# Own buffers for weight sums, the wide down group run from the last row pair to the first, and a fifth place for split weights

## The chip, the cores and the metric

The kernel runs on one core of a Trainium2 chip. The metric is the device time of one execution in microseconds. PE is the matrix engine, PEld its weight load, DVE the vector engine, ACT the scalar engine, POOL is GpSimd, SP the queue from which nearly all loads are issued.

## The reference, cut to what matters

One encoder block: RMSNorm, a combined input projection, two kinds of attention, an output projection with a residual, RMSNorm, and a gated MLP with a residual. All of it is float32. The change touches the MLP alone (256 tokens, `D_MODEL` 2048, `D_FF` 5632):

```
g = x @ w_gate
u = x @ w_up
gc = conv_b + sum over i of conv_w[i] * shifted g
return (jax.nn.silu(gc) * u) @ w_down
```

## The kernel before, in words

**Split weights.** Each float32 weight block is cut into a high part, which ACT writes (`whi`, operations of line 250), and a low part, which DVE writes (`wlo = weight - whi`, line 254). PE then multiplies each block two or three times (high by high, low by high, high by low). A split weight stands in a *place*: one `whi` tile and one `wlo` tile of 128x1024. There are four places (`his`, `los`, lines 320 and 321), filled in turn, and a place is free again when PE has used it. So ACT, DVE and PE form a pipeline: ACT writes the high part of a piece, DVE the low part behind it, PE uses both.

**Raw weights.** They come from DRAM by SP into buffers of the pool `raws` (line 319): five tiles `raw`, later one `more_raw` (line 1879), and, as the activations `hl` die, eight halves of the tiles `halves0` to `halves3` (`hl_free`, line 740). A buffer is free again when the low parts of all that it holds are written.

**Row pairs.** The MLP's down projection runs for most columns by a scheme with seven products for each 2x2 block of tiles. `RowPair` (line 376) is one such block row: its weights, and sums of its weight quarters, are multiplied with the activations (`act`) or with sums of activation quarters (`S`, "sums of values"). The weight sums are made by DVE into a buffer of `raws` (`weight_sums`, line 613; `sums`, `two` and `more` in the code), which is claimed in `load_pair` (line 575) together with the buffers of the loads. The values' sums `S` are made on DVE and ACT when the activations are finished (`value_sums`, line 1954), saved to DRAM (`save_sums`, line 1974) and loaded again into `sin0`, `sin1` or `sums0` (the pool `s_parts`) by `load_S` (line 560) before the pair needs them. Part of the weight sums of the wide group is made in DRAM long before by accumulating DMAs (`early0` to `early21`) and loaded like weights.

**The stages.** Attention fills the first 400 us or so. Then come gate and up tiles, part of them in five groups of the seven-product scheme ("quads" below, weights `w_up_s`); then the "mid" group (`w_down_m`, 22 row pairs, 512 columns); then the "wide" group (`w_down_s`, 22 row pairs, 1024 columns, four pieces a pair), from 948 us on. Between the pieces of the wide group stand pieces of four more column tiles of `w_down` ("others"). Both groups need the values' sums of all 22 pairs, so each is loaded from DRAM twice; only those of the last two pairs go from their making straight to the mid group.

**What sets the order.** Each engine runs its instructions in the order in which they were written out. A planner at build time writes them: threads (the functions with `yield`) claim buffers from pools (`Slots`), wait for events, and are served by modelled costs. `LANDING` (line 67) is the planner's constant for how long a load takes to land. The planner's times decide nothing at run time; only the order that comes out, and the waits that the shared buffers bring, do.

**Outputs.** `mid_out` (line 2194) ends the mid group: DVE combines seven banks into a buffer, ACT scales, POOL adds the residual (line 278), POOL issues two stores. `down_out` (line 2008) does the like for each of the four other column tiles, in two tiles `mt` of the pool `mts` (12 tiles of 128x258), from which POOL stores. `scheme_out` (line 2233) ends the kernel.

Of the kernel before, what the change touches and what calls it, by code (L numbers as in the profile page):

```python
# [15 lines left out]
P = 128  # L16
# [49 lines left out]
COPY_PACE, COPY_AT, SUMS_AT = 6000.0, 14, 48  # L66
LANDING, SAVING = 2600.0, 2500.0
BEHIND = 3
MID_LEAD, TAIL = 4, "mmdmmddddmmddd"
LAST = FC // 2 - 1  # L70
# [147 lines left out]
def encoder_block(ctx: ExitStack, tc: tile.TileContext, io):  # L218
# [11 lines left out]
    def tiles(pool, n, shape, name, dt=F32):  # L230
        return [pool.tile(shape, dt, tag=f"{name}{i}", name=f"{name}{i}") for i in range(n)]
# [90 lines left out]


    combined = Slots(tiles(wpool, 1, [P, PW], "sums"))

# [50 lines left out]
    class RowPair:  # L376
# [50 lines left out]
        def used(self, kind):  # L427
            self.left[kind] -= 1
            if self.left[kind] == 0:
                fl.put(raws, self.at[kind])  # L430

    s_parts = Slots([])
    pieces = []
# [125 lines left out]
    def load_pair(r):  # L559
        def load_S():  # L560
            if r.near:
                r.ev_S = ev_near[r.g]
                return
            if r.of == "mid" and r.g in last_S:
                yield last_S[r.g][1]
                r.S = last_S[r.g][0][0]
                fl.set(r.ev_S)
                return
            r.S = yield from one(s_parts)
            src, saved = saved_sums["up" if r.of == "up" else "down"][r.g]  # L570
            yield saved
            yield "sp", 600
            load(r.S, src, r.ev_S, nc.sync)

        q = r.q
        if r.wide:
# [36 lines left out]
    def weight_sums(r):  # L613
        yield r.loaded
        q = r.q
        if r.wide:
            low, up, t, m = (r.at[k] for k in ("lower", "upper", "two", "more"))
            if r.mode == "both":
                yield r.summed[0]
                yield from TT(m[:, :q], low[:, :q], t[:, :q], ALU.add)  # L620
                yield from TT(m[:, q:], m[:, :q], low[:, q:], ALU.add)
                fl.set(r.summed[1])
                r.used("two")
            else:
                yield r.first_loaded
# [1246 lines left out]
    near, ev_near = [None] * (KC // 2), [Event() for _ in range(KC // 2)]  # L1872
    act = mts = None

    def mlp_buffers():

        nonlocal act, mts
        yield ev_s2t
# [3 lines left out]
        act = mpool.tile([P, FC, 2, SEQ], F32R, name="act")  # L1882
        mts = Slots(tiles(mpool, 12, [P, NT], "mt"))
        for t in tiles(mpool, 2, [P, PW], "sin"):
            fl.put(s_parts, t)
        for t in tiles(mpool, 1, [P, PW], "more_raw"):
            fl.put(raws, t)
        for b in banks[4:]:
# [65 lines left out]
    def value_sums(dst, saved, a, b, place=None):  # L1954
# [152 lines left out]
    def scheme_products(p, r):  # L2107
# [31 lines left out]
        if p is r.pieces[-1]:  # L2139
            if not r.near:  # L2140
                if r.S is not near[-1]:
# [302 lines left out]
```

## Time and profile before

| what | value |
|---|---|
| time, median of 3 runs | 1107.14 us (1105.82 to 1108.59) |
| the profiled execution | 1107.99 us |
| its span, first to last instruction | 1106.0 us |
| granted TensorE clock | 1.000 |
| DVE busy in the span | 1016.9 us (92%) |
| ACT busy | 750.8 us (68%) |
| POOL busy | 149.6 us (14%) |
| loads, stores and copies | 265.35 MB, mean 240 GB/s |

The profile is a page of one execution and the views that its trace answers: busy times in chosen stretches, waits (who waited for whom), a timeline of single instructions, and the DMAs from issue to landing. In a row of the timeline the columns are start and duration in us, engine, line of the code, operation, output and inputs by the program's names without their numbers, shape, and a count where equal rows were merged; in brackets stands idle time ahead of it, with what ended it. Starts are the better measure of pace: an instruction's shown duration overlaps the next one's by some 0.1 us on DVE, and by 0.17 us on PE.

### The profile page before, as it was taken

Reading aid. Unit: us, or ns where it says so; the run is one execution under the profiler, and the core shown is the slowest. Engines: PE = TensorE matmul, PEld = TensorE weight load, DVE = VectorE, ACT = ScalarE, POOL = GpSimd, SP = SyncE. Lnnn points to the kernel's source line nnn. Section 1 sums busy time; section 2 is a strip of 40 time slices with the busy share of each in tenths; the row PEclk is TensorE's granted clock in tenths of the full one; section 3 lists DMA queues with packets and bytes.
Section 4 is the critical chain, followed back from the end, with each engine's and each line's share of the span. In section 5 each row is a group of like instructions: output and inputs, shape, how many; then the busy total and the mean of one; then the engine's idle time right before and its main releaser. Section 6 shows DMA issues by size and latency. Waiting matters only on the chain.

```text
span 1106.0 us, 22349 instructions
## 1 busy us (share of the span) xinstructions
PE 1095.7 (99%) x8164; PEld 1046.2 (95%) x8164; DVE 1016.9 (92%) x1922; ACT 750.8 (68%) x1514; POOL 149.6 (14%) x217
## 2 busy tenths in 40 slices
PE   9999999999999999999999999999999999999998
PEld 9999999999999999999999999999999999887777
DVE  8979888888878989999999999999999998999997
ACT  8788979798647776656656666665666665766664
POOL 3211222322433400000000000000000000304011
PEclk9999999999999999999999999999999999999999
DMA  8765678667877887665747668667888879699891
GB/s 325 253 230 175 194 226 228 173 195 183 257 204 209 237 283 270 213 205 184 255 161 227 208 208 276 216 220 258 277 307 295 286 260 359 233 337 318 274 313 62
DMA packets 82470, 265.35 MB, mean 240 GB/s; under 512 B 9304, under 2 KB 13016, under 8 KB 82360
## 3 DMA queue, kind: packets, MB, share of 16 engines
q1 hardware_dynamic: 78600, 254.08, 67.6%
q0 software_dynamic: 3472, 9.57, 5.4%
q8 instruction: 64, 1.05, 0.4%
q14 instruction: 46, 0.38, 0.1%
q10 hardware_dynamic: 288, 0.27, 0.1%
HBM read 245.39 MB, written 35.13 MB: 254 GB/s over the span
## 4 chain that ended last, share of the span: by engine, by line
PE 83%; DVE 7%; ACT 4%; DMA 3%; issue 2%; POOL 0%; DVEq 0%; SPq 0%; ACTq 0%; POOLq 0%
PE bank L290 23%; PE bank L713 15%; PE bank L714 15%; PE bank L715 15%; PE bank L2040 10%; PE bank L2041 5%; DVE wlo L254 4%; PE bank L296 2%; ACT whi L250 1%; DMA raw<-early 1%; DVE scr L262 1%; ACT scr L250 1%; DMA raw<-in_w_cq 1%; DMA halves<-early 1%; DVE halves L254 1%
## 5 line engine op out<-in xcount | busy, mean ns | idle before, releaser
L250 ACT ACTIVATE whi<-raw 128x512 fp32r<-128x512 f32 (+2 forms) x513 | 383.0, 767 | 152.4 <-PE bank L714 48.7
L254 DVE TENSOR_TENSOR wlo<-raw,whi 128x512 fp32r<-128x512 f32 (+2 forms) x513 | 445.1, 886 | 29.1 <-ACT whi L250 25.4
L713 PE MATMUL bank<-hl,whi 128*128 128x258 f32 (+1 forms) x1208 | 347.7, 288 | 0.0
L714 PE MATMUL bank<-hl,whi 128*128 128x258 f32 (+1 forms) x1208 | 343.7, 285 | 0.0
L715 PE MATMUL bank<-hl,wlo 128*128 128x258 f32 (+1 forms) x1208 | 343.3, 284 | 0.2
L715 PEld LDWEIGHTS bank<-hl,wlo 128*128 128x128 f32 x1208 | 229.7, 190 | 1.0 <-DVE wlo L254 0.6
L714 PEld LDWEIGHTS bank<-hl,whi 128*128 128x128 f32 x1208 | 229.3, 190 | 0.1
L713 PEld LDWEIGHTS bank<-hl,whi 128*128 128x128 f32 x1208 | 228.3, 189 | 0.4
L290 PE MATMUL bank<-whi,act 128*128 128x256 f32 (+1 forms) x600 | 152.9, 306 | 0.0
L2040 PE MATMUL bank<-hl,whi 128*128 128x512 f32 x384 | 136.5, 395 | 0.0
L290 PEld LDWEIGHTS bank<-whi,act 128*128 128x128 f32 x600 | 105.0, 189 | 6.2
L2041 PE MATMUL bank<-hl,wlo 128*128 128x256 f32 x384 | 107.6, 280 | 0.0
L278 POOL TENSOR_TENSOR mt<-mt,mt 128x256 f32<-128x256 f32 x3 | 13.5, 4496 | 646.6 <-ACT mt L250 646.6
L290 PE MATMUL bank<-wlo,act 128*128 128x256 f32 (+1 forms) x300 | 91.7, 306 | 0.0
L2040 PEld LDWEIGHTS bank<-hl,whi 128*128 128x128 f32 x384 | 72.1, 188 | 14.8
L250 ACT ACTIVATE whi<-halves 128x1024 fp32r<-128x1024 f32 (+1 forms) x68 | 62.4, 933 | 34.1 <-PE bank L290 16.7
L290 PE MATMUL bank<-whi,sin 128*128 128x256 f32 (+1 forms) x264 | 76.3, 333 | 0.0
L254 DVE TENSOR_TENSOR wlo<-halves,whi 128x1024 fp32r<-128x1024 f32 (+1 forms) x68 | 72.9, 1099 | 2.9 <-ACT whi L250 2.8
L2041 PEld LDWEIGHTS bank<-hl,wlo 128*128 128x128 f32 x384 | 72.4, 189 | 0.0
L250 ACT ACTIVATE whi<-more_raw 128x1024 fp32r<-128x1024 f32 (+2 forms) x58 | 49.9, 871 | 25.1 <-PE bank L714 9.3
L290 PEld LDWEIGHTS bank<-wlo,act 128*128 128x128 f32 x300 | 56.7, 189 | 2.8
L254 DVE TENSOR_TENSOR wlo<-more_raw,whi 128x1024 fp32r<-128x1024 f32 (+2 forms) x58 | 57.0, 994 | 2.4 <-ACT whi L250 2.4
(311 smaller groups left out, 2163.1 us busy)
## 6 DMA issues: line engine op xcount, KB each, us to landing
raw<-in_w_gate SPq DMA_DIRECT2D x74, 512.0 KB, 4.8
raw<-in_w_in SPq DMA_DIRECT2D x52, 512.0 KB, 4.9
raw<-in_w_up SPq DMA_DIRECT2D x43, 512.0 KB, 4.9
raw<-in_w_up_s SPq DMA_DIRECT2D x34, 512.0 KB, 4.4
raw<-in_w_out SPq DMA_DIRECT2D x32, 512.0 KB, 5.3
sin<-s_down SPq DMA_DIRECT2D x30, 512.0 KB, 6.5
s_down<-sums SPq DMA_DIRECT2D x22, 512.0 KB, 4.4
raw<-in_w_down_m SPq DMA_DIRECT2D x18, 512.0 KB, 5.5
```

The costliest lines, as they stand in the source:

```text
L250: nc.scalar.activation(out, in_, f, **kw)
L254: nc.vector.tensor_tensor(out, a, b, op)
L262: nc.vector.scalar_tensor_tensor(out, a, s, b, op0, op1)
L278: nc.gpsimd.tensor_tensor(out, a, b, op)
L290: nc.tensor.matmul(o, l, r, start=start, stop=stop)
L296: nc.tensor.transpose(o, i, ident[:n, :n])
L713: nc.tensor.matmul(ps, whi, xhi, start=start, stop=False)
L714: nc.tensor.matmul(ps, whi, xlo, start=False, stop=False)
L715: nc.tensor.matmul(ps, wlo, xhi, start=False, stop=stop)
L2040: nc.tensor.matmul(ps, whi, x, start=start, stop=False)
L2041: nc.tensor.matmul(ps[:, :n], wlo, x[:, 0, :], start=False, stop=stop)
```

## The change

1. **Own buffers for weight sums.** A new pool `made` takes `more_raw` and the two halves of `halves3`; `raws` keeps the five `raw` tiles and the other six halves. The sums' buffers are claimed from `made` when DVE is to make the sums, and no longer from `raws` when the pair's load is planned. The number of buffers is the same.
2. **The wide group runs from pair 21 to pair 0**, and the values' sums of pairs 19, 20 and 21, which the mid group used last, stay on chip for the wide group's first three pairs. Three loads of `s_down` and two saves go away, 512 KB each.
3. **A fifth place.** The 12 tiles `mt` are cut from three tiles of four. Behind `mid_out`, `mts_to_ring` takes all 12, gives four back, and turns the other two tiles into a fifth `whi` and a fifth `wlo` (`whi_more`, `wlo_more`). In the wide group, `down_out` has four `mt` where it had twelve.
4. `LANDING` in the planner goes from 2600 to 3200 ns.

The counts of computing instructions stay the same on every engine. PE's order is the same up to the first wide product; from there on the pairs come in the other order, and the others' pieces stand at somewhat other points among them.

The planner writes all engines' orders anew, and three places show what that does. In the rows, `waits` names the engines or DMA queues whose semaphores a row waits for (DMAHW are SP's transfers, DMASW POOL's), numbers behind a name tell buffers apart, and the instruction's line is one higher after the change.

The first place is DVE in the fourth quad, around the low part `wlo1` of a pair. Before:

```order
L254 TENSOR_TENSOR wlo0_89<-raw1_81,whi0_85 128x1024 [waits PE_49,Activation_49]
L254 TENSOR_TENSOR more_raw0_5458<-raw0_80 128x512 [waits DMAHW6_49]
L254 TENSOR_TENSOR more_raw0_5458<-raw0_80,more_raw0_5458 128x256 [waits DVE_49]
L254 TENSOR_TENSOR more_raw0_5458<-more_raw0_5458,raw0_80 128x256 [waits DVE_49]
L254 TENSOR_TENSOR wlo1_90<-raw4_84,whi1_86 128x1024 [waits DMAHW4_49,Activation_49]
L254 TENSOR_TENSOR wlo2_91<-raw0_80,whi2_87 128x512 [waits PE_49,Activation_49]
L254 TENSOR_TENSOR wlo2_91<-raw0_80,whi2_87 128x256 [waits PE_49,Activation_49]
L254 TENSOR_TENSOR sums0_93<-mt5_5449,sums0_93 128x256 [waits DMAHW5_49]
```

And with the change:

```order
L255 TENSOR_TENSOR wlo0_89<-more_raw0_5449,whi0_85 128x1024 [waits PE_49,Activation_49]
L255 TENSOR_TENSOR sums0_93<-mt1_5445,sums0_93 128x256 [waits DMAHW5_49,Activation_49]
L255 TENSOR_TENSOR more_raw0_5449<-raw0_80 128x512 [waits DMAHW6_49,DVE_49]
L255 TENSOR_TENSOR more_raw0_5449<-raw0_80,more_raw0_5449 128x256 [waits DVE_49]
L255 TENSOR_TENSOR more_raw0_5449<-more_raw0_5449,raw0_80 128x256 [waits DVE_49]
L255 TENSOR_TENSOR wlo1_90<-raw1_81,whi1_86 128x1024 [waits DMAHW4_49,Activation_49]
L255 TENSOR_TENSOR wlo2_91<-raw0_80,whi2_87 128x512 [waits PE_49,Activation_49]
L255 TENSOR_TENSOR wlo2_91<-raw0_80,whi2_87 128x256 [waits PE_49,Activation_49]
```

A row of `value_sums` (`sums0<-mt`) has moved from behind the three low parts to ahead of them. The same stands in the second and third quad.

The second place is DVE in the wide group, from the row that frees a buffer for a load of `early` sums to the row that reads that load. Before, for pair 16: the low part from `halves1` in the first row frees it, SP's load of `early16` goes into it, and the last row reads it.

```order
L254 TENSOR_TENSOR wlo1_90<-halves1_11086,whi1_86 128x1024 [waits Activation_49]
L254 TENSOR_TENSOR wlo2_91<-more_raw0_5458,whi2_87 128x1024 [waits DMAHW4_49,Activation_49]
L254 TENSOR_TENSOR wlo3_92<-raw0_80,whi3_88 128x512 [waits Activation_49]
L254 TENSOR_TENSOR halves0_11043<-raw3_83 128x512 [waits DMAHW4_49,DMAHW3_49]
L254 TENSOR_TENSOR halves0_11043<-halves0_11043,raw1_81 128x512 [waits DMAHW1_49,DVE_49]
L254 TENSOR_TENSOR wlo0_89<-raw2_82,whi0_85 128x1024 [waits Activation_49]
L254 TENSOR_TENSOR wlo1_90<-raw4_84,whi1_86 128x512 [waits DMAHW7_49,Activation_49]
L254 TENSOR_TENSOR halves3_11164<-halves0_11043,raw1_81 128x512
L254 TENSOR_TENSOR more_raw0_5458<-halves3_11164,halves1_11086 128x512 [waits DMAHW6_49,DMAHW1_49]
```

With the change, the pair whose load has the fewest rows between is pair 5. The row ahead of these twelve (a low part from `halves1`) frees the buffer, and the last one reads it:

```order
L255 TENSOR_TENSOR wlo1_90<-halves2_11117,whi1_86 128x512 [waits DMAHW4_49,Activation_49]
L255 TENSOR_TENSOR more_raw0_5449<-halves3_11155,raw0_80 128x512
L255 TENSOR_TENSOR wlo2_91<-raw1_81,whi2_87 128x1024 [waits Activation_49]
L255 TENSOR_TENSOR wlo3_92<-raw3_83,whi3_88 128x1024 [waits DMAHW6_49,Activation_49]
L255 TENSOR_TENSOR wlo_more_11455<-halves3_11155,whi_more_11454 128x1024 [waits Activation_49]
L255 TENSOR_TENSOR wlo0_89<-raw0_80,whi0_85 128x1024 [waits Activation_49]
L255 TENSOR_TENSOR wlo1_90<-halves2_11117,whi1_86 128x1024 [waits Activation_49]
L255 TENSOR_TENSOR wlo2_91<-halves3_11155,whi2_87 128x1024 [waits Activation_49]
L255 TENSOR_TENSOR halves3_11155<-halves0_11034 128x512 [waits DMAHW6_49,DMAHW3_49,DVE_49]
L255 TENSOR_TENSOR halves3_11155<-halves3_11155,halves0_11034 128x512 [waits DVE_49]
L255 TENSOR_TENSOR wlo3_92<-more_raw0_5449,whi3_88 128x512 [waits PE_49,Activation_49]
L255 TENSOR_TENSOR more_raw0_5449<-halves1_11078 128x512 [waits DMAHW3_49,DMAHW2_49,DVE_49]
```

Eight rows lay between freeing and reading, counted with the reading one; now it is twelve, and twelve to 23 for the other pairs from 18 down. Before, the pairs 14, 16, 18, 19 and 21 had eight to ten.

The third place is DVE where the fifth place is first filled, nine rows behind the last one of `mid_out`'s combination of the banks:

```order
L255 TENSOR_TENSOR wlo0_89<-raw2_82,whi0_85 128x1024 [waits Activation_49]
L255 TENSOR_TENSOR wlo1_90<-halves0_11034,whi1_86 128x512 [waits DMAHW0_49,Activation_49]
L255 TENSOR_TENSOR more_raw0_5449<-halves3_11155,halves1_11078 128x512
L255 TENSOR_TENSOR wlo2_91<-halves0_11034,whi2_87 128x1024 [waits Activation_49]
L255 TENSOR_TENSOR wlo3_92<-raw4_84,whi3_88 128x1024 [waits DMAHW2_49,Activation_49]
L255 TENSOR_TENSOR wlo_more_11455<-halves3_11155,whi_more_11454 128x1024 [waits DMASW6_49,Activation_49,Pool_49]
L255 TENSOR_TENSOR wlo0_89<-halves1_11078,whi0_85 128x1024 [waits Activation_49]
```

The row of `wlo_more` waits for POOL and for the POOL queue's store of the first `down_out` (DMASW6), which reads from the `mt` tiles that become the place. Such a wait did not stand here before.

The core of the diff:

```diff
-LANDING, SAVING = 2600.0, 2500.0
+LANDING, SAVING = 3200.0, 2500.0
+RING_AT = 5
+    made = Slots([])
...
-                fl.put(raws, self.at[kind])
+                by_sums = kind in ("more", "sums") or kind == "two" and self.mode == "third"
+                fl.put(made if by_sums else raws, self.at[kind])
...
-        for g in range(FC // 2):
+        order = range(FC // 2) if of == "mid" else range(LAST, -1, -1)
+        for g in order:
             r = RowPair(src[g], g, q, of)
-            r.first, r.last, r.near = g == 0, g == LAST, False
+            r.first, r.last, r.near = g == order[0], g == order[-1], False
...
+            if r.of == "down" and r.g > LAST - 3:
+                yield ev_kept[r.g]
+                r.ev_S = kept_S[r.g].ev_S
+                r.S = kept_S[r.g].S
                 return
...
-            r.at["two"], r.at["more"] = yield raws, 2
             if r.mode == "both":
+                r.at["two"] = yield from one(raws)
...
-            r.at["raw"], r.at["sums"] = yield raws, 2
+            r.at["raw"] = yield from one(raws)
...
+            if r.mode == "both":
+                yield r.summed[0]
+                r.at["more"] = yield from one(made)
+            else:
+                yield r.first_loaded
+                r.at["two"], r.at["more"] = yield made, 2
...
-        t, raw = r.at["sums"], r.at["raw"]
+        t = r.at["sums"] = yield from one(made)
...
-            fl.put(raws, t[:, a : a + PW])
+            fl.put(raws if 2 * i + a // PW < 8 - 2 else made, t[:, a : a + PW])
...
-        mts = Slots(tiles(mpool, 12, [P, NT], "mt"))
+        mt_rows[:] = tiles(mpool, 3, [P, 4 * NT], "mt")
+        mts = Slots([t[:, i * NT : (i + 1) * NT] for t in mt_rows for i in range(4)])
...
-        fl.spawn(save_sums(dst, saved, parts, place is None and not last))
+        if not last:
+            fl.spawn(save_sums(dst, saved, parts, place is None))
...
+    def mts_to_ring():
+        yield mts, 12
+        yield scheme[RING_AT][0].ready[0]
+        for i in range(4):
+            fl.put(mts, mt_rows[0][:, i * NT : (i + 1) * NT])
+        for i, (slots, name) in enumerate(((his, "whi_more"), (los, "wlo_more"))):
+            t = mpool.tile([P, 4 * NT], F32R, tag=f"mt{i + 1}", name=name)
+            fl.put(slots, t[:, :PW])
...
+        fl.spawn(mts_to_ring())
```

More of the change, by code (lines that the diff above doesn't have):

```diff
@@ L429, in used @@
             if self.left[kind] == 0:
-                fl.put(raws, self.at[kind])
-    s_parts = Slots([])
+                by_sums = kind in ("more", "sums") or kind == "two" and self.mode == "third"
+                fl.put(made if by_sums else raws, self.at[kind])
+    s_parts, kept_S = Slots([]), {}
+    ev_kept = {g: Event() for g in range(LAST - 2, LAST + 1)}
     pieces = []
@@ L567, in load_S @@
                 fl.set(r.ev_S)
+                kept_S[r.g] = r
+                fl.set(ev_kept[r.g])
+                return
+            if r.of == "down" and r.g > LAST - 3:
+                yield ev_kept[r.g]
+                r.ev_S = kept_S[r.g].ev_S
+                r.S = kept_S[r.g].S
                 return
             r.S = yield from one(s_parts)
+            if r.of == "mid" and r.g > LAST - 3:
+                assert r.S is not near[-1]
+                kept_S[r.g] = r
+                fl.set(ev_kept[r.g])
             src, saved = saved_sums["up" if r.of == "up" else "down"][r.g]
@@ L616, in weight_sums @@
         if r.wide:
+            if r.mode == "both":
[4 more added lines that the diff above has]
+                r.at["two"], r.at["more"] = yield made, 2
             low, up, t, m = (r.at[k] for k in ("lower", "upper", "two", "more"))
             if r.mode == "both":
-                yield r.summed[0]
                 yield from TT(m[:, :q], low[:, :q], t[:, :q], ALU.add)
@@ L624, in weight_sums @@
             else:
-                yield r.first_loaded
                 yield from TT(m[:, :q], up[:, :q], up[:, q:], ALU.add)
@@ L633, in weight_sums @@
             return
-        t, raw = r.at["sums"], r.at["raw"]
+        t = r.at["sums"] = yield from one(made)
+        raw = r.at["raw"]
         if r.mode == "third":
@@ L1872, in encoder_block @@
     near, ev_near = [None] * (KC // 2), [Event() for _ in range(KC // 2)]
-    act = mts = None
+    act = mts = mpool = None
+    mt_rows = []
     def mlp_buffers():
-        nonlocal act, mts
+        nonlocal act, mts, mpool
         yield ev_s2t
@@ L1886, in mlp_buffers @@
         for t in tiles(mpool, 1, [P, PW], "more_raw"):
-            fl.put(raws, t)
+            fl.put(made, t)
         for b in banks[4:]:
@@ L2140, in scheme_products @@
             if not r.near:
-                if r.S is not near[-1]:
+                if kept_S.get(r.g) is r:
+                    pass
+                elif r.S is not near[-1]:
                     fl.put(s_parts, r.S)
```

## The prediction

> **What bounds the kernel now.** I read the stretches first: busy time of each engine in chosen windows (core, window, length, then PE, PEld, DVE, ACT and POOL with their counts, the granted clock, the DMA share and GB/s).
>
> ```profile
> 640.00:720.00 80.00, 80.00 (x640) 78.47 (x639) 78.72 (x146) 50.22 (x81) 0.00 (x0) 1.00 0.70 233
> 800.00:900.00 100.00, 100.00 (x751) 95.98 (x750) 92.31 (x162) 61.01 (x96) 0.00 (x0) 1.00 0.83 286
> 900.00:948.00 48.00, 48.00 (x318) 43.91 (x318) 43.95 (x71) 28.04 (x42) 3.35 (x4) 1.00 0.88 319
> 948.00:1000.00 52.00, 52.00 (x241) 42.43 (x240) 51.77 (x58) 37.02 (x45) 12.86 (x8) 1.00 0.85 301
> 1000.00:1025.00 25.00, 24.29 (x116) 19.78 (x115) 24.86 (x28) 15.58 (x17) 7.09 (x4) 1.00 0.93 314
> 1025.00:1050.00 25.00, 23.88 (x114) 19.46 (x113) 22.60 (x26) 14.81 (x16) 0.00 (x0) 1.00 0.79 271
> 1050.00:1075.00 25.00, 22.84 (x111) 18.33 (x110) 23.27 (x26) 15.85 (x20) 5.33 (x4) 1.00 0.89 300
> ```
>
> PE is full up to 1000 us at a granted clock of 1.00, so nothing can be won there, only lost. From 1000 to 1075, in the wide group, it is not, while DVE is busy 99% of one window and has holes in the next two. So PE and DVE bound this stage together. Next I read who waited: PE from 780 us on, then DVE from 940 us on.
>
> ```profile
> PE bank L290 <- DVE wlo L254: 4.0, 5, 1.1
> ```
>
> ```profile
> DVE more_raw L254 <- DMA halves<-early: 2.3, 1, 2.3
> DVE halves L254 <- DMA raw<-early: 1.5, 1, 1.5
> ```
>
> PE waits for the low parts five times, and DVE waits twice for a load of `early` sums. The timeline shows the five, and that DVE's two waits stand in front of two of them.
>
> ```profile
> 1037.31 0.69 DVE L254 TENSOR_TENSOR halves<-halves,raw 128x512 f32<-128x512 f32 x1
> 1040.30 0.69 DVE L254 TENSOR_TENSOR more_raw<-halves,halves 128x512 f32<-128x512 f32 x1 [2.30 <-DMA halves<-early]
> ```
>
> ```profile
> 1054.18 0.69 DVE L254 TENSOR_TENSOR halves<-raw,raw 128x512 f32<-128x512 f32 x1 [1.51 <-DMA raw<-early]
> ```
>
> ```profile
> 1010.89 0.50 PE L290 MATMUL bank<-wlo,sin 128*128 128x512 f32 x1 [0.71 <-DVE wlo L254]
> ```
>
> ```profile
> 1040.44 0.39 PE L290 MATMUL bank<-whi,act 128*128 128x512 f32 x1
> 1040.66 0.39 PE L290 MATMUL bank<-whi,sums 128*128 128x512 f32 x1
> 1042.18 0.50 PE L290 MATMUL bank<-wlo,sums 128*128 128x512 f32 x1 [1.12 <-DVE wlo L254]
> ```
>
> ```profile
> 1056.07 0.50 PE L290 MATMUL bank<-wlo,sin 128*128 128x512 f32 x1 [1.08 <-DVE wlo L254]
> ```
>
> ```profile
> 1065.86 0.51 PE L290 MATMUL bank<-wlo,sin 128*128 128x512 f32 x1 [0.55 <-DVE wlo L254]
> 1068.74 0.50 PE L290 MATMUL bank<-wlo,sin 128*128 128x512 f32 x1 [0.53 <-DVE wlo L254]
> ```
>
> Undisturbed, a matmul starts about 0.22 us behind the one ahead (1040.44 to 1040.66) though it is shown 0.39 long. A bracket thus hides 0.17 us, and the five cost 4.0 + 5 x 0.17 = 4.85 us. That is all the change can win; PE's work does not change.
>
> **The change part by part.**
>
> *Loads earlier (own buffers for sums).* The load that DVE waits for at 1040.30 was issued here:
>
> ```profile
> 1032.62 0.33 SPq L543 DMA_DIRECT2D halves<-early  x1
> ```
>
> It landed 7.7 us later; in before's order only eight DVE rows lie between the row that frees its buffer and the one that reads it. From 948 to 1000 DVE does 58 rows in 51.77 us, 0.89 us each, so eight rows are 7.1 us: too few. With the change at least twelve rows lie between, an estimate of 10.7 us by the same 0.89, and most loads have more. The two DMA waits should go, and with them the stalls at 1042.18 and 1056.07: 1.12 + 1.08 + 2 x 0.17 = 2.54 us. What is late next is DVE itself.
>
> *DVE's own lag.* The other three stalls cost 0.71 + 0.55 + 0.53 + 3 x 0.17 = 2.3 us. Each stands behind adds on POOL; the first has no DMA wait ahead of it at all:
>
> ```profile
> 994.58 0.69 DVE L254 TENSOR_TENSOR halves<-halves 128x512 f32<-128x512 f32 x1
> 995.18 1.82 DVE L254 TENSOR_TENSOR wlo<-raw,whi 128x1024 fp32r<-128x1024 f32 x2
> ...
> 1002.67 0.68 DVE L254 TENSOR_TENSOR more_raw<-halves,halves 128x512 f32<-128x512 f32 x1
> 1003.39 1.11 DVE L254 TENSOR_TENSOR more_raw<-more_raw,halves 128x512 f32<-128x512 f32 x1
> ```
>
> ```profile
> 993.79 10.16 POOL L278 TENSOR_TENSOR mt<-mt,mt 128x256 f32<-128x256 f32 x1 [34.09 <-ACT mt L250]
> 1004.03 1.08 POOL L278 TENSOR_TENSOR mt<-mt,s 128x256 f32<-128x256 f32 x1
> ```
>
> A sum of this shape takes 0.68, but 1.11 beside POOL's add. The change leaves these POOL adds where they are. It also makes more DVE rows wait for the row just ahead of them: nine more in the wide stage, because three buffers serve all sums. Such a row starts 0.72 us behind (1002.67 to 1003.39) instead of 0.60 (994.58 to 995.18), so nine cost 9 x 0.12 = 1.1 us. Against it stands the fifth place: DVE and ACT can run one split further ahead, about 1.1 us. Also, the last two stalls, 9 and 12 us behind the one at 1056.07, met a lead that the DMA waits had used up. Bounds of what remains: 0 us, and 2.3 + 1.1 = 3.4 us. I take 1.3, nearer the lower end, since two of the three stalls lose part of their cause.
>
> *Fewer transfers.* Three loads of `s_down` and two saves, 512 KB each, vanish: 2.6 MB.
>
> ```profile
> sin<-s_down SPq DMA_DIRECT2D x30, 512.0 KB, 6.5
> s_down<-sums SPq DMA_DIRECT2D x22, 512.0 KB, 4.4
> ```
>
> PE waits for none of them before, so by themselves they cost nothing and give nothing; at the 301 GB/s of the window from 948 us they free 8.7 us of transfer time for other loads. That is in the term above; bounds 0 and 0. The buffers that hold the kept sums are free again after the first three wide pairs, and the loads that wait for them are used three pairs later.
>
> *The quads.* Here PE is full, but the low part comes just in time in every quad. Of three quads the DVE row with that low part (the first of three merged) and PE's first use of it:
>
> ```profile
> 606.51 2.15 DVE L254 TENSOR_TENSOR wlo<-raw,whi 128x1024 fp32r<-128x1024 f32 x3
> ...
> 740.21 2.16 DVE L254 TENSOR_TENSOR wlo<-raw,whi 128x1024 fp32r<-128x1024 f32 x3
> 742.28 0.42 DVE L254 TENSOR_TENSOR sums<-mt,sums 128x256 fp32r<-128x256 f32 x1
> 742.62 1.22 DVE L254 TENSOR_TENSOR wlo<-raw,whi 128x1024 fp32r<-128x1024 f32 x1
> ```
>
> ```profile
> 607.90 0.28 PE L715 MATMUL bank<-hl,wlo 128*128 128x258 f32 x1
> ```
>
> ```profile
> 674.63 0.39 PE L715 MATMUL bank<-hl,wlo 128*128 128x258 f32 x1
> ```
>
> ```profile
> 741.49 0.39 PE L715 MATMUL bank<-hl,wlo 128*128 128x258 f32 x1
> ```
>
> A 128x1024 split is 1.22 long, so that of 606.51 ends 0.17 us ahead of PE's use, and that of 740.21 (741.43) 0.06 ahead. In the order after the change the row `sums<-mt` stands ahead of this split instead of behind: 0.34 us more on DVE (742.28 to 742.62). PE then loses 0.17 at 607.90, 0.28 at 741.49, and about as much at 674.63, whose matmul shows the same 0.39 as that of 741.49: 0.73 us. In the first quad the lead is 0.38, and nothing is lost. Bounds: 0, if DVE starts this run of rows earlier than before; and 2.1 us, if the moved row, which waits for ACT and for an earlier save, also costs a wait of the size of such a row in each of three quads (3 x 0.7).
>
> *The mid group.* DVE has thirteen more rows that wait for the one just ahead: 13 x 0.12 = 1.6 us, hidden in the 7.7 and 4.1 us that DVE is idle from 800 to 900 and from 900 to 948. Bounds 0 and 1.6; I take 0, since PE is full there with room.
>
> *Sum.* -4.85 + 1.3 + 0.73 = -2.8 us: a span of 1103.2 instead of 1106.0, an execution of 1105.2 instead of the profiled 1107.99. That execution lay 0.85 us above the median of the runs, 1107.14; the forecast is on the median: **1104.3 us**. The unknowns at their best give 1107.14 - 4.85 = 1102.3, at their worst 1107.14 - 4.85 + 3.4 + 2.1 + 1.6 = 1109.4.
>
> **The rivals.**
>
> *All stalls go and the quads lose nothing:* 1102.3. For it speaks the fifth place and loads that come well ahead; against it, the POOL adds and the moved rows, which are seen in trace and order.
>
> *DVE is the bound, and the stalls come back elsewhere.* DVE's 24.86 of 25 us from 1000 to 1025, with PE at 24.29 and not one DMA wait, speak for it: places and early loads do not make DVE faster. Then 3.4 us remain, with the quads at 0.73 to 2.1: 1107.14 - 4.85 + 3.4 + 1.4 = 1107.1, no change. Against it: DVE's holes of 2.4 and 1.7 us in the next two windows, which are what the change fills. The Trainium skill (page "Perfetto Trace Analysis", section "Identifying the Most-Contended Engine") takes occupancy as a fair measure of an engine's distance to its limit for VectorE, and tells to work on that engine first; by it the 99% row would leave this rival as the forecast, and the two windows with holes are where trace and rule part.
>
> *The fifth place makes DVE wait for POOL: slower.* Its first `wlo_more` row waits for the store of the first `down_out`. Before, POOL's rows there were quick; the second fence is the landing of the stores to `outT`, the third the DVE row that stands where the first `wlo_more` will:
>
> ```profile
> 944.13 1.25 POOL L278 TENSOR_TENSOR mt<-mt,mt 128x256 f32<-128x256 f32 x1 [558.71 <-ACT mt L250]
> ...
> 947.92 0.63 POOL L2026 DMA_DIRECT2D outT<-mt  x1 [0.36 <-POOL mt L278]
> ```
>
> ```profile
> DMA to landing us min/median/max: 2.1/5.3/6.0
> ```
>
> ```profile
> 957.51 0.68 DVE L254 TENSOR_TENSOR wlo<-more_raw,whi 128x512 fp32r<-128x512 f32 x1
> ```
>
> The store lands by 947.92 + 6.0 = 953.9; the `wlo_more` row has as many DVE rows ahead of it as before's row of 957.51, 3.6 us later. But the same add took 10.16 us at 993.79. If it does so here, everything is 8.9 us later, DVE waits 5.3 us, and with the 1.0 us that lead covered at 1042.18 (2.30 waited, 1.29 lost) PE loses 4.3: 1104.3 + 4.3 = 1108.6. It decides from 4.6 us of delay on. `mid_out`'s stores, behind which SP's next load now stands, would be as late and could add more. Against it: PE's order, and so the time of that `down_out`, is the same up to there. The Trainium skill (page "SBUF — State Buffer", section "Who interferes with whom") says that a DVE instruction with two SBUF inputs contends with a GpSimd instruction that reads SBUF, and that whichever issued first blocks the other fully for its whole instruction. The trace agrees in kind, with the 10.16 us, but not in size on DVE's side, which lost 0.43 us at 1003.39 to an add of 1.08; by the rule's full block that row would lose some 1.1, and the sum would be about 2 us higher over the three groups of adds.
>
> *The loads don't come earlier,* because SP's queue stands still behind a load that waits for `mid_out`'s stores: DVE's waits stay, and only the quads' 0.73 is new: 1107.9.
>
> **How the numbers follow.** Forecast 0.45, all stalls gone 0.13, DVE the bound 0.17, POOL's wait 0.18, loads held 0.07. About 0.3% (3.3 us) is what a measurement of this kernel can tell from no change: the line to faster lies at 1103.8, to slower at 1110.5. Faster by more: all of the second case and about half of the forecast's, whose own spread is 1102.8 to 1106: 0.35. Slower by more: two thirds of POOL's case, where the late stores add to it, and a fifth of the cases of DVE and of the held loads, where delays pile up: 0.17. Within: 0.48. The range from 1101.5 to 1110.5 takes in the bounds and the rivals.
>
> **What would show it.** PE's idle brackets for low parts in the wide stage fall from five to one or two of under 1 us; DVE shows no wait for `early` after 948; the L715 matmuls at about 608, 675 and 741 start late by 0.2 to 0.3; the first `wlo_more` has no wait for POOL. A DMA wait of DVE in the quads, PE short of full before 948, or stalls that stay with a DVE without holes would make it wrong.

## The result and the profile after

The changed kernel takes 1103.26 us (median of 7 runs, 1102.62 to 1103.95); the kernel before took 1108.59 in the same comparison (1105.82 to 1109.28). The ratio is 0.9957, with a 95% interval of 0.9947 to 0.9967: 0.43% or 4.8 us faster, where 2.8 had been forecast (the two medians lie 5.3 us apart; the ratio and its interval are used below). The profiled span is 1101.3 us, 4.7 less than before.

The stretches of the changed kernel's wide group, in the columns of the prediction's first fence:

```profile
948.00:1000.00 52.00, 51.53 (x237) 41.89 (x236) 51.76 (x58) 36.08 (x44) 11.27 (x11) 1.00 0.86 301
1000.00:1025.00 25.00, 25.00 (x120) 20.74 (x119) 24.90 (x29) 15.69 (x18) 0.00 (x0) 1.00 0.92 311
1025.00:1050.00 25.00, 25.00 (x119) 20.74 (x118) 24.79 (x30) 16.52 (x18) 0.00 (x0) 1.00 0.82 293
1050.00:1075.00 25.00, 25.00 (x123) 20.90 (x123) 24.93 (x27) 17.53 (x22) 12.80 (x4) 1.00 0.91 332
```

PE (the second number) is now full from 1000 to 1075 us, and DVE (the fourth pair) has lost its holes there. PE's waits from 780 us on are one, and DVE's waits from 940 us on name no load any more (the waits for PE and ACT that remain lie before 948 and after 1080 us):

```profile
PE bank L291 <- DVE wlo L255: 0.5, 1, 0.5
```

```profile
DVE mt L255 <- PE bank L736: 2.7, 1, 2.7
DVE wlo L255 <- ACT whi L251: 2.3, 2, 1.9
DVE wlo_more L255 <- ACT whi_more L251: 0.2, 1, 0.2
```

The one wait that is left, on PE's timeline, and what lies ahead of it on DVE and POOL:

```profile
998.78 0.40 PE L291 MATMUL bank<-whi,sin 128*128 128x512 f32 x1
999.64 0.50 PE L291 MATMUL bank<-wlo,sin 128*128 128x512 f32 x1 [0.47 <-DVE wlo L255]
```

```profile
995.19 1.66 DVE L255 TENSOR_TENSOR wlo<-raw,whi 128x1024 fp32r<-128x1024 f32 x1
996.77 1.23 DVE L255 TENSOR_TENSOR halves<-raw,halves 128x512 f32<-128x512 f32 x1
997.93 1.66 DVE L255 TENSOR_TENSOR wlo<-halves,whi 128x1024 fp32r<-128x1024 f32 x1
```

```profile
994.33 1.44 POOL L279 TENSOR_TENSOR mt<-mt 128x256 f32<-128x256 f32 x1 [34.65 <-ACT mt L251]
995.85 1.61 POOL L279 TENSOR_TENSOR mt<-mt,s 128x256 f32<-128x256 f32 x1
997.53 0.97 POOL L279 TENSOR_TENSOR mt<-mt,res 128x256 f32<-128x256 f32 x1
```

Beside POOL's three adds, two of DVE's splits take 1.66 instead of 1.22 us and a sum 1.23 instead of 0.69. By starts, with the 0.23 us that lies between two undisturbed matmuls here, the stall is 999.64 - 998.78 - 0.23 = 0.63 us.

Since PE's order is the same up to the wide group, the starts of the same matmuls in the two traces show in which stage the time came. The three longest stages, in us:

| stage (starts of the same matmuls) | before | after |
|---|---|---|
| quads (the 4101st to the 6201st) | 267.20 | 266.85 |
| mid group (to the first wide product) | 169.25 | 169.24 |
| wide group (first wide product to the last matmul) | 153.29 | 148.76 |

The wide group gave 4.53 us, the quads 0.35, the mid group nothing (0.01). Attention, up to 395 us, varied by up to 2.5 us between the profiled executions of all the kernels below although its code is the same in all; so stages, not spans, are compared between single traces, and ratios between runs. A stage's time is from one trace of each kernel; how far it varies from execution to execution is not known, but kernels with the same order there agree in the quads within 0.11 us (made_only and p_made).

### The profile page after: what moved, and what is told of

It reads as the page before. It is cut to its first block, busy times and chain, and to the rows that moved or that the text cites. A ratio compares the mean times of both kernels' runs of the same rounds, so it can differ in the third digit from the quotient of the medians.

```text
span 1101.3 us, 22419 instructions
## 1 busy us (share of the span) xinstructions
PE 1094.4 (99%) x8164; PEld 1046.1 (95%) x8164; DVE 1015.2 (92%) x1922; ACT 753.8 (68%) x1514; POOL 147.6 (13%) x217
## 5 line engine op out<-in xcount | busy, mean ns | idle before, releaser
L251 ACT ACTIVATE whi<-raw 128x512 fp32r<-128x512 f32 (+2 forms) x493 | 353.1, 736 | 159.4 <-PE bank L735 53.7
L255 DVE TENSOR_TENSOR wlo<-raw,whi 128x512 fp32r<-128x512 f32 (+2 forms) x493 | 407.4, 847 | 30.6 <-ACT whi L251 29.7
L291 PE MATMUL bank<-whi,act 128*128 128x256 f32 (+1 forms) x574 | 143.5, 302 | 0.0
L251 ACT ACTIVATE whi<-more_raw 128x1024 fp32r<-128x1024 f32 (+1 forms) x72 | 74.1, 1029 | 39.8 <-DVE more_raw L255 22.7
L279 POOL TENSOR_TENSOR mt<-mt 128x256 f32<-128x256 f32 x3 | 12.2, 4083 | 653.0 <-ACT mt L251 653.0
L255 DVE TENSOR_TENSOR wlo<-more_raw,whi 128x1024 fp32r<-128x1024 f32 (+1 forms) x72 | 85.6, 1189 | 3.2 <-ACT whi L251 3.1
L291 PE MATMUL bank<-wlo,act 128*128 128x256 f32 (+1 forms) x287 | 86.8, 302 | 0.0
L291 PE MATMUL bank<-whi,sin 128*128 128x256 f32 (+1 forms) x250 | 70.0, 325 | 0.0
L251 ACT ACTIVATE whi<-halves 128x1024 fp32r<-128x1024 f32 (+2 forms) x54 | 50.6, 955 | 20.9 <-PE bank L291 8.2
L255 DVE TENSOR_TENSOR wlo<-halves,whi 128x1024 fp32r<-128x1024 f32 (+2 forms) x54 | 59.2, 1122 | 0.5 <-ACT whi L251 0.3
```

Source lines behind the costliest of these rows:

```text
L251: nc.scalar.activation(out, in_, f, **kw)
L255: nc.vector.tensor_tensor(out, a, b, op)
L279: nc.gpsimd.tensor_tensor(out, a, b, op)
L291: nc.tensor.matmul(o, l, r, start=start, stop=stop)
```

## The experiments

Twelve kernels in three groups. All ratios are to the kernel before, run beside them; what two kernels of different groups differ by is taken from their ratios. The waits are the sums of the brackets in one trace; by starts each stall is some 0.17 us longer.

| kernel | ratio (95%) | quads | wide group | PE's waits for low parts from 780 us | DVE's waits for loads in the wide group |
|---|---|---|---|---|---|
| before | 1 | 267.20 | 153.29 | 4.0 | 4.0 |
| the change | 0.9957 (0.9947 to 0.9967) | 266.85 | 148.76 | 0.5 | 0 |
| made_only | 1.0002 (0.9993 to 1.0011) | 267.88 | 152.06 | 2.3 | 0 |
| rev_only | 0.9996 (0.9987 to 1.0005) | 267.15 | 152.50 | 2.1 | 2.3 |
| ring_only | 1.0007 (0.9998 to 1.0016) | 267.17 | 154.41 | 4.5 | 4.3 |
| land_only | 0.9989 (0.9980 to 0.9997) | 267.15 | 151.55 | 2.3 | 1.1 |
| no_ring | 0.9979 (0.9970 to 0.9987) | 266.84 | 150.45 | 0.6 | 0 |
| no_made | 0.9976 (0.9967 to 0.9985) | 266.89 | 150.79 | 2.2 | 1.4 |
| no_rev | 0.9978 (0.9970 to 0.9987) | 266.85 | 150.29 | 1.2 | 0 |
| no_land | 0.9971 (0.9961 to 0.9981) | 268.05 | 148.79 | 0.5 | 0 |
| p_before | 0.9974 (0.9964 to 0.9984) | 267.18 | 151.61 | 2.0 | 5.2 |
| p_made | 0.9975 (0.9965 to 0.9984) | 267.99 | 149.39 | 0.6 | 0 |
| p_after | 0.9950 (0.9935 to 0.9965) | 266.85 | 148.02 | 0 | 0 |
| late_pool | 1.0039 (1.0024 to 1.0054) | 266.85 | 157.75 | 6.7 | 5.9 (a store) |

**One part alone.** The kernel before, with one of the change's four parts.

made_only, the own buffers (all lines with `made` or `by_sums`), of which the core is

```diff
+    made = Slots([])
...
-            r.at["two"], r.at["more"] = yield raws, 2
             if r.mode == "both":
+                r.at["two"] = yield from one(raws)
...
+            if r.mode == "both":
+                yield r.summed[0]
+                r.at["more"] = yield from one(made)
```

> Only the own buffers for weight sums, in the kernel before. Theory A (the loads come earlier, so DVE no longer waits for early sums): both DMA waits of DVE in the wide stage go, with the stalls of 1.12 and 1.08 us behind them, 2.0 to 3.0 us faster, and the three stalls behind POOL's adds remain. Theory B (the fifth place is what covers the stalls): 0 to 0.7 us faster, five stalls remain. Theory C (the transfers that vanish make room): no change, DMA waits remain.

DVE's waits for loads are gone, as Theory A had it, but the kernel is no faster, where that theory had 2.0 to 3.0 us: 1108.23 us against 1108.04. PE's three large stalls that remain:

```profile
965.04 0.50 PE L290 MATMUL bank<-wlo,sums 128*128 128x512 f32 x1 [0.60 <-DVE wlo L254]
...
1013.17 0.51 PE L290 MATMUL bank<-wlo,sin 128*128 128x512 f32 x1 [0.82 <-DVE wlo L254]
...
1078.77 0.50 PE L290 MATMUL bank<-wlo,sums 128*128 128x512 f32 x1 [0.90 <-DVE wlo L254]
```

The second and the third stand behind the two `down_out` of the wide group on POOL:

```profile
995.51 10.61 POOL L278 TENSOR_TENSOR mt<-mt,mt 128x256 f32<-128x256 f32 x1 [34.84 <-ACT mt L250]
...
1061.19 11.56 POOL L278 TENSOR_TENSOR mt<-mt,mt 128x256 f32<-128x256 f32 x1 [51.37 <-ACT mt L250]
```

So the wide group won only 1.2 us, and the quads lost 0.7; what is left is less than this comparison can tell (1.0 us to either side).

rev_only, the reversed order with the three kept sums of values:

```diff
-        for g in range(FC // 2):
+        order = range(FC // 2) if of == "mid" else range(LAST, -1, -1)
+        for g in order:
...
+            if r.of == "down" and r.g > LAST - 3:
+                yield ev_kept[r.g]
+                r.ev_S = kept_S[r.g].ev_S
+                r.S = kept_S[r.g].S
```

> Only the reversed order of the wide pairs with the three kept sums of values, in the kernel before. Theory A: within 1 us of before, loads are as close to their use as before. Theory B: the same. Theory C: 5 transfers fewer, DVE's waits for early sums shrink from 3.8 to under 1 us, 2 to 3 us faster.

Theory C expected the waits for `early` sums to fall under 1 us and a gain of 2 to 3 us; those waits fell to 1.7 (2.3 with one for another load), and the time did not change beyond its interval.

ring_only, the fifth place (`mts_to_ring`, the tiles `mt` in three rows):

```diff
+        fl.spawn(mts_to_ring())
```

> Only the fifth place, in the kernel before. Theory A: DVE still waits 2 to 4 us for early sums; the place covers at most one split (1.1 us) of each, so 1 to 2.5 us faster. Theory B: nearly all of the gain, 3.5 to 5 us faster. Theory C: no change.

Theory B falls with this run: the place alone removes no stall. Nor is it 1 to 2.5 us faster, as A had it; the time is unchanged. DVE waited twice for loads of `early` sums, 2.2 and 1.8 us:

```profile
DVE halves L255 <- DMA raw<-early: 2.2, 1, 2.2
DVE raw L255 <- DMA halves<-early: 1.8, 1, 1.8
```

A place further ahead is of no use when the raw weights have not landed.

land_only, the planner's constant:

```diff
-LANDING, SAVING = 2600.0, 2500.0
+LANDING, SAVING = 3200.0, 2500.0
```

> Only the planner's constant for landing, 3200 instead of 2600, in the kernel before. Theories A, B and C: within 1 us of before. A fourth, that the planner's later landing alone spaces loads and uses: 2 us or more faster.

0.9989 is 1.2 us faster, with an interval that holds the 1 us of Theories A to C; the fourth theory's 2 us did not come. Yet the constant alone took the waits for `early` away and left one of 1.1 us for another load.

Added up, the four parts alone make -0.06%; together they make -0.43%. So they are worth more together than alone, and the next group leaves one out.

**The change without one part.** The edits are those of the first group, taken back from the changed kernel.

no_ring:

```diff
-        fl.spawn(mts_to_ring())
```

> The change without the fifth place. Theory A (early loads are enough): within 0.5 us of the changed kernel. Theory D (DVE needs as long as PE in the wide stage, each of its lags reaches PE unless a lead covers it, so loads in time and a longer lead are needed together): DVE has no wait for DMA, but 2 to 4 stalls of 0.5 to 1 us remain, 1.5 to 3 us slower than the changed kernel. Theory E (the gain is the luck of one order): anything.

0.9979 against 0.9957: 2.4 us slower than the change. No wait for a load, but the wide group is 1.7 us longer, in two stalls of about 0.5 us by starts and a dozen of at most 0.2 us. Loads in time are not enough, which is against A and for D in kind and in time; D's stalls of 0.5 to 1 us came out at the lower end, and the small ones it did not have.

no_made:

```diff
+            r.at["two"], r.at["more"] = yield raws, 2
             if r.mode == "both":
-                r.at["two"] = yield from one(raws)
```

> The change without the own buffers for sums. Theory A: DVE waits again 1.5 us or more for early sums, 2 to 4 us slower than the changed kernel. Theory D: the same waits, of which the fifth place covers about one split each, 1 to 3 us slower. Theory B (the place covers them): within 0.5 us.

2.1 us slower than the change, as both A and D had it. The waits are back, 1.4 us instead of before's 4.0:

```profile
DVE raw L255 <- DMA halves<-early: 1.0, 1, 1.0
DVE raw L255 <- DMA raw<-early: 0.4, 1, 0.4
```

D expected the fifth place to cover about one split of each wait. It did not cover the longer one: that wait ends at 1072.23 us, and the stall of PE behind it, at 1074.84, is 1.5 us by starts.

no_rev:

```diff
-        order = range(FC // 2) if of == "mid" else range(LAST, -1, -1)
-        for g in order:
+        for g in range(FC // 2):
```

> The change with the wide pairs in the old order and the sums of values loaded again. Theories A and D: no DMA wait of DVE, within 1 us of the changed kernel. Theory C (the 5 transfers matter): DMA waits of 1 us or more come back, 1.5 to 3 us slower.

2.3 us slower, where A and D had less than 1. It isn't Theory C either, which had the time right, since no DVE wait for a load came back. PE waits three times instead of once:

```profile
PE bank L291 <- DVE wlo L255: 0.5, 1, 0.5
PE bank L723 <- DVE wlo_more L255: 0.4, 1, 0.4
PE bank L2051 <- DVE wlo_more L255: 0.3, 1, 0.3
```

What in the reversed order saves these is open: it changes at once which kind of pair comes first, where the others' pieces stand, and how many transfers there are.

no_land:

```diff
-LANDING, SAVING = 3200.0, 2500.0
+LANDING, SAVING = 2600.0, 2500.0
```

> The change with the old planner constant for landing. Theories A, C and D: within 1 us of the changed kernel, since own buffers give the loads more time than either constant. The fourth theory (the constant spaces the loads): 2 us or more slower, with DMA waits of DVE.

1.6 us slower, where A, C and D had less than 1 and the fourth theory 2 or more with DMA waits; the intervals of this ratio and the change's just overlap, so the trace has to say where it lies. None of it is in the wide group (148.79 us) and no DMA wait came back. It is in the quads, 268.05 instead of 266.85. DVE and PE in the second quad:

```profile
604.64 0.42 DVE L255 TENSOR_TENSOR sums<-mt,sums 128x256 fp32r<-128x256 f32 x1
...
606.11 0.42 DVE L255 TENSOR_TENSOR sums<-mt,sums 128x256 fp32r<-128x256 f32 x1
...
607.97 2.16 DVE L255 TENSOR_TENSOR wlo<-raw,whi 128x1024 fp32r<-128x1024 f32 x3
```

```profile
608.95 0.28 PE L735 MATMUL bank<-hl,whi 128*128 128x258 f32 x1
609.25 0.39 PE L736 MATMUL bank<-hl,wlo 128*128 128x258 f32 x1
```

Two rows of `sums` stand ahead of the just-in-time split, which ends at 609.19. PE starts its use 0.30 us behind the matmul ahead instead of 0.12: a loss such as the prediction expected of the change, in this kernel and not in the changed one. The table shows that own buffers and the old constant together do it: the three kernels with both (made_only, p_made, no_land) take 267.88 to 268.05 us in the quads, all others 266.84 to 267.20.

**POOL's adds.** p_before, p_made and p_after leave out the three POOL adds of each of the three `down_out` that use POOL, in the kernel before, in made_only and in the changed kernel. The planner's costs stay, so the other engines' orders are the same.

```diff
-            yield from PTT(o_, t[:, :SEQ], o_, ALU.add)
+            yield "pool", 90 + 3.9 * SEQ
             fl.put(mts, t)
-            yield from PTT(o_, o_, s_2[:, :SEQ], ALU.mult)
-            yield from PTT(o_, o_, hT[ST + m][:, :SEQ], ALU.add)
+            yield "pool", 90 + 3.9 * SEQ
+            yield "pool", 90 + 3.9 * SEQ
```

> The kernel before without the three POOL adds of each of the three POOL-side down_out (their column tiles lack scale and residual); the other engines' orders are the same. Theory P (a DVE row beside a POOL add takes longer, and that lag is what reaches PE): the stall at about 1010 us goes, the last two shrink by half or more, the two behind DMA waits stay; 1 to 2.3 us faster than before. Theory Q (DVE is short of time whatever POOL does): five stalls of the same size, within 0.5 us.

0.9974, 2.9 us faster than before, more than Theory P's 1 to 2.3. The stall at 1010 is gone, and those at 1066 and 1069 too; two behind DMA waits stay, and a smaller one came at 1074, behind a third DMA wait:

```profile
PE bank L290 <- DVE wlo L254: 2.0, 3, 1.0
```

> The kernel with only the own buffers for sums, without the same POOL adds. Theory P: of its three large stalls (964, 1012 and 1077 us) the two behind down_out's adds go, the one behind mid_out's adds stays; 2 us faster than with them, some 1106.2 us. Theory Q: all three stay, 1108.

1105.46 us and 0.9975: by the ratios 3.0 us faster than made_only. The two stalls behind `down_out` are gone; that of 965, behind `mid_out`'s adds, which were kept, stays:

```profile
PE bank L290 <- DVE wlo L254: 0.6, 1, 0.6
```

> The changed kernel without the same POOL adds. Theory P: its one stall of 0.6 us at 999 goes, some 0.6 us faster, 1102.7 us. Theory Q: it stays, 1103.3.

1102.44 us, 0.8 us less than the change: its last stall is gone, and PE waits for no low part at all from 780 us on. The intervals of the two ratios overlap; the trace, not the time, decides here. Theory P holds in all three: the stalls behind `down_out` come from its adds on POOL, and the others stay.

late_pool, the changed kernel with POOL kept busy ahead of the store on which the fifth place waits:

```diff
             yield from PTT(o_, o_, hT[ST + m][:, :SEQ], ALU.add)
+            for op in (ALU.add, ALU.subtract) * (6 if m == 0 else 0):
+                nc.gpsimd.tensor_tensor(o_, o_, hT[ST + m][:, :SEQ], op)
```

> The changed kernel with six more pairs of adding and subtracting the residual on POOL in the first down_out, ahead of its store, some 9 to 12 us of POOL. If the fifth place's first use waits for that store, as the slower rival of the prediction has it: DVE (or ACT ahead of it) waits 3 to 6 us at the first wlo_more, PE loses 2 to 5 us, 1105.5 to 1109 us. If the store is covered or doesn't matter: within 0.7 us of 1103.3.

1112.23 us, slower than expected: 1.0039 of before and 9 us over the change. The added rows took 14.96 us and not 9 to 12. The store, the wait of the first `wlo_more`, and PE's:

```profile
947.97 14.96 POOL L2045 TENSOR_TENSOR mt<-mt,res 128x256 f32<-128x256 f32 x12
963.29 0.63 POOL L2052 DMA_DIRECT2D outT<-mt  x1 [0.36 <-POOL mt L2045]
```

```profile
965.77 1.23 DVE L255 TENSOR_TENSOR wlo_more<-halves,whi_more 128x1024 fp32r<-128x1024 f32 x1 [5.88 <-DMA outT<-mt]
```

```profile
956.24 0.39 PE L291 MATMUL bank<-whi,sums 128*128 128x512 f32 x1
958.26 0.50 PE L291 MATMUL bank<-wlo,sums 128*128 128x512 f32 x1 [1.63 <-DVE wlo L255]
...
962.64 0.40 PE L291 MATMUL bank<-whi_more,sums 128*128 128x512 f32 x1
967.05 0.68 PE L291 MATMUL bank<-wlo_more,sums 128*128 128x512 f32 x1 [4.01 <-DVE wlo_more L255]
```

The wait that the slower rival described is real: 5.88 us on DVE, 967.05 - 962.64 - 0.23 = 4.18 on PE. The longer loss has two more parts. The POOL adds slowed DVE beside them before the wait (splits took 1.74 to 1.77 us there instead of 1.22), 958.26 - 956.24 - 0.23 = 1.79 us on PE. And after the wait PE was slow for a while, 1.6 us in all, which the last section shows. The three make 7.6 of the 9.0 us that the wide group is longer; the rest is in smaller stalls.

## Why the prediction was right, and where it was not

The time and the direction were right, 1104.3 forecast and 1103.26 measured; the gain was 4.8 us, not 2.8. That the time came nearer than the gain is partly luck: the forecast started from 1107.14 us for the kernel before, which took 1108.59 in the comparison. By stages, the wide group was forecast to give 4.85 - 1.3 = 3.55 us and gave 4.53, and the quads were forecast to cost 0.73 and gave 0.35. By its steps:

*Loads earlier* was right. The two waits for `early` sums and the stalls behind them went, and none of the kernels with own buffers has such a wait (late_pool's is for a store), while all those without have 1.1 to 5.2 us. But the price given to this step, 2.54 us, is not what it is worth alone: made_only shows no gain. In the wide group, where DVE is as full as PE, the time given back in the two waits was spent at the next lags, two of which stand behind POOL's adds. Without these adds the own buffers shorten the wide group by 151.61 - 149.39 = 2.2 us (p_before and p_made, single traces), near the price.

*DVE's own lag* was right in its cause and too large in size: 1.3 us taken, 0.63 measured. p_before, p_made and p_after show the cause, POOL's adds. no_ring shows the cover: without the fifth place the wide group is 1.7 us longer, more than the 1.1 us that the prediction counted for it. ring_only and no_made show its limit: alone, or behind a load that comes late, the place covers nothing.

*The quads* failed. The step was that the row `sums<-mt`, which the order puts ahead of the just-in-time split, makes PE lose 0.73 us. PE lost nothing there and won 0.35. Two of the places in the changed kernel:

```profile
604.76 0.42 DVE L255 TENSOR_TENSOR sums<-mt,sums 128x256 fp32r<-128x256 f32 x1
...
606.62 2.16 DVE L255 TENSOR_TENSOR wlo<-raw,whi 128x1024 fp32r<-128x1024 f32 x3
```

```profile
608.20 0.28 PE L735 MATMUL bank<-hl,whi 128*128 128x258 f32 x1
608.32 0.28 PE L736 MATMUL bank<-hl,wlo 128*128 128x258 f32 x1
```

```profile
740.05 2.15 DVE L255 TENSOR_TENSOR wlo<-raw,whi 128x1024 fp32r<-128x1024 f32 x3
```

```profile
741.63 0.28 PE L736 MATMUL bank<-hl,wlo 128*128 128x258 f32 x1
```

The first split ends at 607.84, 0.48 us ahead of its use, where before it was 0.17; the second ends 0.36 ahead, where before it was 0.06. The prediction counted rows only from the split two rows up, as if DVE started there at the same time as before. DVE does not wait for PE there; it runs through, so rows further up count too. From one such split to that of the next quad DVE runs 121 rows in every kernel here, and six of them are `sums<-mt`, before as after: the moved row adds nothing to a quad. What counts is how long a whole quad takes DVE. By the starts of the splits that was (740.21 - 606.51) / 2 = 66.85 us before and is (740.05 - 606.62) / 2 = 66.72 after; PE's uses of them lie 66.80 and 66.66 apart. So in before DVE was a little slower than PE can be, its lead shrank from quad to quad, and PE lost the difference; with the change DVE keeps up.

A part of this is rows that wait for the row just ahead of them, which the trace shows with 0.03 us of idle time: 26 in a quad before, 25 after, 27 in no_land. The prediction gives such a row 0.12 us and counted them for the wide and the mid group, but not for the quads. The count goes with the planner's constant, to which the prediction gave no price: with the new constant it is 25 in all the kernels here, with the old one 26, or 27 where the sums have own buffers. One row is an estimate of 0.12 us a quad, which is less than what before lost; the rest is not explained. With the old constant and own buffers (no_land) the lead is gone, and the loss is there, 0.18 us by starts at 609.25, and 1.2 us over all the quads.

*The mid group* at 0 was right: 169.25 and 169.24 us. *Fewer transfers* at 0 could not be told from the reversed order; no_rev is 2.3 us slower, without a DMA wait, so the two edits together are worth something, beside the other parts, that the prediction did not price.

*The rivals.* The loads did come earlier. DVE is at 24.90, 24.79 and 24.93 of 25 us, and PE is full beside it: both are at their limit now, so the Trainium skill's rule on occupancy (page "Perfetto Trace Analysis", section "Identifying the Most-Contended Engine") pointed at the right engine, but there were 4.5 us to win in the wide group before that limit was reached. The wait for POOL did not come: the store was issued at 947.89, as early as before. The prediction had DVE wait from 3.6 us of delay on, and PE lose from 4.6 on; by late_pool, where 963.29 - 947.89 = 15.4 us of delay gave 5.88 of waiting on DVE, DVE waits from about 9.5 us on. Two numbers made the difference: the store landed in about 2.5 us (963.29 to 965.77) and not in the 6.0 that the prediction took from the longest, and the waiting row itself came later, at 959.9 instead of the changed kernel's 956.4, since DVE was slowed by the same adds.

*The rule on the shared port.* The Trainium skill (page "SBUF — State Buffer", section "Who interferes with whom") has a DVE instruction with two SBUF inputs and a GpSimd one that reads SBUF block each other fully. With POOL's adds left out the stalls behind them go, which agrees in kind; that a port is the cause, no run here separates from other causes. In size a split beside POOL's adds took 1.66 instead of 1.22 us, 0.44 more, which is less than the length of any of those adds (0.97 to 1.61); the estimate of 2 us more that the prediction drew from a full block did not come. On POOL's side the block could last far longer than one DVE instruction, as the last section shows.

## What to carry to other kernels

Where two engines run at par, as PE and DVE do in this wide group, the waits of the trace need not add up to what their removal wins: removing one can only move PE to the next lag, and four edits that win 0.06% in sum when each stands alone won 0.43% together. Price such a stage by what the slower engine still loses over all of it (late loads, a neighbour that slows it, dependent rows) and by the lead that can cover it. A moved row of an in-order engine is priced from the last place where that engine really waited, not from a few rows above; in a stage that repeats, that is the engine's time for a whole round.

## What the runs showed of the hardware that was not expected

After PE had stood still for 4.2 us in late_pool, it ran slower for some 3.5 us: the granted clock (third number from the end) was 0.66 in the stretch of 5 us behind the wait, and 0.50 from 967.5 to 970.5.

```profile
962.00:966.00 4.00, 1.03 (x6) 0.61 (x4) 0.23 (x1) 0.00 (x0) 3.13 (x6) 1.00 0.27 96
966.00:971.00 5.00, 3.95 (x10) 3.16 (x11) 5.00 (x4) 1.31 (x2) 3.78 (x4) 0.66 0.38 138
971.00:976.00 5.00, 5.00 (x23) 4.04 (x22) 4.93 (x8) 3.21 (x4) 0.00 (x0) 1.00 0.96 324
```

```profile
968.80 0.63 PE L291 MATMUL bank<-whi_more,act 128*128 128x512 f32 x1
969.23 0.63 PE L291 MATMUL bank<-whi,sin 128*128 128x512 f32 x1
```

The matmuls start 0.43 us apart instead of 0.23; over the eight from 967.05 to 970.51 that is 970.51 - 967.05 - 8 x 0.23 = 1.6 us on top of the wait. The stalls of up to 1.3 us in the kernel before show nothing of the kind. The Trainium skill (page "TensorE: Matmul & The Clock Gate", Part 1 on the HAM clock gate) says that an idle window of about 3.4 us halves the array's clock until it has been busy for as long; the trace agrees, with 0.43 us between starts, close to twice 0.23, and a recovery within 4 us. So this wait of 4.2 us cost PE 1.6 us more than itself.

The first POOL add of a `down_out`, which reads two `mt` tiles, is very uneven in length. Of the 22 of the second and third `down_out` in the kernels that keep these adds, ten are shown with 9.55 to 11.91 us and twelve with 1.22 to 3.57. What ends a long one can be seen in the changed kernel:

```profile
1059.00 9.55 POOL L279 TENSOR_TENSOR mt<-mt 128x256 f32<-128x256 f32 x1 [59.53 <-ACT mt L251]
```

```profile
1067.38 0.68 DVE L255 TENSOR_TENSOR more_raw<-halves 128x512 f32<-128x512 f32 x1
1068.09 1.01 DVE L255 TENSOR_TENSOR more_raw<-more_raw,halves 128x512 f32<-128x512 f32 x1
```

From the start of the add on, DVE's rows follow each other without a pause and keep their usual length; 1068.09 is the first that waits for the row ahead, with DVE idle for 0.03 us, and the add ends 0.46 us behind its start, while that row takes 1.01 instead of 0.69. In all ten long adds, and in five of the short ones, the end lies 0.46 to 0.57 us behind the start of the first such DVE row (1003.39 and 993.79 + 10.16 in the prediction's rows are another). In the other seven, which took 1.23 to 1.58, the add got through without a pause of DVE; what differs there is open. So in these cases POOL was held off by a whole run of DVE rows, not by one, and got in at a pause of DVE as short as 0.03 us, as far as POOL's spans, which are rough, can tell.
